# A two-block transformer kernel: banks of the wide products, and the engine and place of a blocked substitution

## The chip, the cores and the metric

One core of a Trainium2 chip runs the whole program in one launch. The metric is the time on the device in microseconds (us); lower is better. Three runs of the kernel before gave 936.17, 937.05 and 939.07 us, median 937.05. Engines: TensorE multiplies (PE in the profile, PEld its weight loads), VectorE (DVE), ScalarE (ACT) and GpSimd (POOL) do elementwise work, SyncE (SP) issues most DMA transfers. Each engine runs its own queue strictly in order.

## The reference, cut to what matters

The input is 256 tokens of 1024 numbers, in float32. Two transformer blocks follow each other. The first has an attention with 8 heads, beside it a gated delta rule with 8 heads in chunks of 64 tokens, an output projection and an MLP of width 4096. The second has a short convolution branch, a retention branch, three output projections and a gated MLP of width 2816.

The change touches two places. The first is the delta rule's triangular solve, which is done for each of 32 units (8 heads by 4 chunks):

```python
m = jnp.where(strict, jnp.einsum('bhnid,bhnjd->bhnij', k_beta, kc) * decay, 0.0)
a_mat = m + jnp.eye(C, dtype=jnp.float32)            # C = 64
uw = lax.linalg.triangular_solve(a_mat, rhs, left_side=True, lower=True, unit_diagonal=True)
```

The second is every projection whose result is wanted with channels on the partitions, such as the MLP's `square(relu(h @ w_up))`.

## The kernel before, in words

**Precision and weights.** Each float32 product is made of reduced-precision ones: an operand is split into a high part H and a rest L, and H times H, H times L and L times H are summed. `load_w` (L207 on) does this for 512 KB of weights at a time: a DMA on SP's queue fills `raw` (3 buffers), ScalarE writes `wh` as a copy of it, VectorE writes `wl` as `raw` minus `wh` (6 buffers each). This pair of instructions, called a split below, occurs 287 times; the nth split is the nth call. `GATE_H` and `GATE_L` tie the first few to instructions that they must follow.

**The wide products.** `gemm_wide` (L300) makes 128 output channels for all 256 tokens in one step of sixteen matmuls: eight with 512 moving columns (the high and low part of the activations side by side) and eight with 256. The result is one PSUM bank. ScalarE copies its second half out and VectorE adds the first half; then the bank is free. There are 84 such steps in the program: 24 in the first MLP, 24 in the convolution branch, 36 in the second MLP. All take their bank from `mmps()`, which goes round 3 banks (`BANKS = {"mm": 3, "sd": 3, "at": 2}`). `atps()` goes round 2 more, which the attention, the transposes of a normed row and one group of a head use.

**The substitution.** Each unit's 64x64 matrix is inverted in blocks. Its 128 diagonal blocks of 16x16 go, one for each partition, through DRAM: `m` is written to `md`, and `mb` is read back with a block in each partition's 256 columns. Fifteen steps of forward substitution follow; step j multiplies 15-j rows by j+1 columns and subtracts. The inverse `tb` and its transpose `ub` are written to DRAM (`td`, `ud`) and read back as `T` and `U` in the layout of units (L937 to L943). Two rounds of 64x64 products on TensorE with the masked matrices `b` (for block sizes 16 and 32, L947 on) then complete the inverse. The first of these products has the operands `U` and `b`.

**What sets the order.** The program is written as one stream: a main line (the delta rule) and a generator `side` of other work (the projections, the attention) from which `go(n)` takes pieces with a total of n. `FILL` holds these n. The framework puts each engine's instructions in its queue by a list scheduler that follows the written order among what its own estimate takes to be ready, so neighbours can change places. `after(name)` forbids an instruction to stand ahead of the instruction recorded under that name on the same engine; a name that is not recorded yet has no effect.

Counting the calls of `load_w` along the stream: split 13 is the last ahead of the substitution's lines (L884 on), splits 14 to 17 belong to `FILL[6]` to `FILL[8]`, split 18 (first half of `att_in(1)`) to `FILL[9]` at L944, split 19 (its second half) to `FILL[10]`, splits 20 to 23 to the gate projection `z_in`.

Of the kernel before, what the change touches and what calls it, by code (L numbers as in the profile page):

```python
# [11 lines left out]
F32 = mybir.dt.float32  # L12
F32R = mybir.dt.float32r
AF = mybir.ActivationFunctionType
# [23 lines left out]
GATE_L = ("xs", "xl", "xl", None, "g")  # L38
TAIL = 4
FILL = (1.3, 2.6, 3.9, 7.8, 1.3, 2.6, 1.3, 3.9, 3.9, 2.6, 2.6, 7.8, 2.6, 7.8)  # L40
# [57 lines left out]
def body(ctx: ExitStack, tc: tile.TileContext, I: dict, cst: bass.AP, out: bass.AP, dbg=None):  # L98
    nc = tc.nc
    P = 128  # L100

    def dump(name, ap):
        if dbg is not None:
            dbg(name, ap)
# [10 lines left out]
    def nm(s):  # L115
        uid[0] += 1
        return f"{s}_{uid[0]}"
# [4 lines left out]
    def G2(name, dt=F32, shape=None):  # L122
        return T2(name, dt, shape, "g")
# [7 lines left out]
    def bank(tag):  # L131
        return psum.tile([P, 512], F32, tag=tag, name=nm(tag), bufs=BANKS[tag])

    def mmps():
        return bank("mm")

    def sdps():
        return bank("sd")

    def atps():  # L140
        return bank("at")

    def act(o, i, f, **kw):
        nc.scalar.activation(o, i, f, **kw)  # L144

    def tt(o, a, b, op, eng=None):
        (eng or nc.vector).tensor_tensor(o, a, b, op=op)  # L147
# [4 lines left out]
    MUL, ADD, SUB, MAX = ALU.mult, ALU.add, ALU.subtract, ALU.max  # L152
# [14 lines left out]
    last, started = {}, []  # L167

    @contextmanager
    def after(what):  # L170

        if what in last:
            with tc.issue_after(last[what].ins):
                yield
        else:
            yield
# [26 lines left out]
    def C(name):  # L203
        o, w = COFF[name]
        return CT[o // 512][:, o % 512:o % 512 + w]


    def load_w(w, k0, nk, c0, ncol):
        raw = wpool.tile([P, nk, ncol], F32, tag="raw", name=nm("raw"), bufs=RBUFS)
        nc.sync.dma_start(raw, w[k0 * P:(k0 + nk) * P, c0:c0 + ncol].rearrange("(k p) n -> p k n", p=P))  # L210
        H = wpool.tile([P, nk, ncol], F32R, tag="wh", name=nm("wh"), bufs=WBUFS)
        L = wpool.tile([P, nk, ncol], F32R, tag="wl", name=nm("wl"), bufs=WBUFS)
        n = len(started)
        started.append(1)
        with after(GATE_H[n] if n < len(GATE_H) else None):
            act(H, raw, AF.Copy)
        with after(GATE_L[n] if n < len(GATE_L) else None):
            tt(L, raw, H.bitcast(F32), SUB)
        return H, L

    def mm(o, a, b, start=True, stop=True):
        nc.tensor.matmul(o, a, b, start=start, stop=stop)  # L222
# [34 lines left out]
    def gemm_tok_steps(w, c0, X, evac):  # L257

        ps = [mmps() for _ in range(2)]
        for q in range(4):  # L260
            H, L = load_w(w, 2 * q, 2, c0, 512)
            for t in range(2):
                for k in range(2):
                    kk = 2 * q + k
                    mm3(ps[t], *X.at(kk, t), H[:, k, :], L[:, k, :], kk == 0, kk == 7)
            if q == 3:
                for t in range(2):
                    evac(t, ps[t])
            yield 2.6
# [7 lines left out]
    def piece():  # L277
        for it in list(later):
            it[0] -= 1
            if it[0] <= 0:  # L280
                later.remove(it)
                it[1]()

    def gemm_ch_steps(w, c0, X, evac):

        ps = mmps()
        for f in range(2):
            H, L = load_w(w, 0, 8, c0 + f * P, P)
            o = ps[:, f * 256:(f + 1) * 256]
            for k in range(8):  # L290
                XH, XL = X.at(k)
                mm(o, H[:, k, :], XH, k == 0, False)
                mm(o, H[:, k, :], XL, False, False)
                last["step"] = nc.tensor.matmul(o, L[:, k, :], XH, start=False, stop=k == 7)  # L294
            if f == 1:
                evac(ps)
            piece()
            yield 2.6

    def gemm_wide(w, c0, X, o, then=None):  # L300


        for f in range(2):
            H, L = load_w(w, 0, 8, c0 + f * P, P)
            ps = mmps()
            for k in range(8):
                mm(ps, H[:, k, :], X.both(k), k == 0, False)
                mm(ps[:, :S], L[:, k, :], X.at(k)[0], False, k == 7)
            half = o[:, f * S:(f + 1) * S]
            act(half, ps[:, S:], AF.Copy)  # L310
            tt(half, ps[:, :S], half, ADD)
            if f == 1 and then:
                then()
            piece()
# [57 lines left out]
    def gemm_k(w, nk, X, *a):  # L372
        return GemmK(w, nk).finish(X, *a)
# [136 lines left out]
    def h8(ap):  # L510
        return ap.rearrange("p (h d) -> p h d", h=8)
# [8 lines left out]
    def cb(name):  # L520

        return C(name)[:, None, :].to_broadcast([P, 8, 64])
# [165 lines left out]
    def go(what):  # L688

        while what not in passed if isinstance(what, str) else what > 0:  # L690
            c = next(side, None)
            if c is None:
                return
            if isinstance(c, str):
                passed.add(c)
            elif not isinstance(what, str):
                what -= c
# [10 lines left out]
    H, L = load_w(w_in, 0, 8, 3584, 16)  # L708
# [101 lines left out]
    md, td, ud = (dram.tile([128, BS], F32, name=n) for n in ("md", "td", "ud"))  # L810
# [6 lines left out]
    def in_blocks(d):  # L817

        d = d[:, :]
        return bass.AP(tensor=d.tensor, offset=d.offset, ap=[[BS, P], [64, 16], [1, 16]])  # L820


    KBE, KD, KT_, MM, BL = [], [], [], [], []
# [61 lines left out]
    tb, ub, mb, tmp = (z_.rearrange("p (i j) -> p i j", i=16) for z_ in (tb_, ub_, mb_, tmp_))  # L885
    nc.gpsimd.tensor_copy(tb_, C("eye16"))
    nc.sync.dma_start(mb, in_blocks(md))
    for j in range(15):
        n, w = 15 - j, j + 1
        tt(tmp[:, :n, :w], mb[:, j + 1:, j:j + 1].to_broadcast([P, n, w]),  # L890
           tb[:, j:j + 1, :w].to_broadcast([P, n, w]), MUL, nc.gpsimd)
        tt(tb[:, j + 1:, :w], tb[:, j + 1:, :w], tmp[:, :n, :w], SUB, nc.gpsimd)
    last["sub"] = nc.gpsimd.tensor_copy(ub, tb.rearrange("p i j -> p j i"))
    nc.sync.dma_start(in_blocks(td), tb)
    nc.sync.dma_start(in_blocks(ud), ub)
    for t in range(2):
        bl = []
        for s in (16, 32):
            b = G2("b")
            with after("sub"):  # L900
                tt(h8(b), h8(MM[t]), cb(f"lev{s}"), MUL, nc.gpsimd)
            bl.append(b)
        BL.append(bl)

# [29 lines left out]
        VB.append(vb)  # L934
    go(FILL[8])

    U, T = [None] * 2, [None] * 2  # L937
    for t in range(2):
        T[t], U[t] = G2("T"), G2("U")
# [1 line left out]
            for c in range(2):  # L941
                nc.sync.dma_start(h8(o)[c * 64:(c + 1) * 64], in_units(d, t, c))
        dump(f"u16{t}", U[t])  # L943
    go(FILL[9])  # L944
    for si, s in enumerate((16, 32)):
        q, pt = [None] * 2, [None] * 2
        for t in range(2):  # L947
            ps = sdps()
            b, u0 = BL[t][si], U[t]
# [66 lines left out]
    for t in range(2):  # L1016
        po = sdps()
        vn = USB[t]
        for c in range(2):
            n = 2 * t + c  # L1020
# [43 lines left out]
    ps = wout.ps  # L1064
# [22 lines left out]
    for i in range(4, 16):  # L1087
        hf = G2("hf")

        def up_evac(i=i, hf=hf):  # L1090
            r = G2("relu")
            act(r, hf, AF.Relu)
            stt(hf, hf, 0.0, r, MAX, MUL)
            hv = hf.rearrange("p (j n) -> p j n", j=2)
            act(hid.h[i], hv, AF.Copy)
            tt(hid.l[i], hv, hid.h[i].bitcast(F32), SUB)

        gemm_wide(I["w_up"][0], 256 * i, X, hf, up_evac)
# [14 lines left out]
    ps = gemm_k(I["w_down"][0], 32, hid, TAIL_DOWN)  # L1113
# [45 lines left out]
    for h in range(4):  # L1159
        ps = sdps()  # L1160
# [33 lines left out]
    for h in range(4):  # L1194
        for t in range(2):
            ps = sdps()
# [25 lines left out]
    for i in range(4):  # L1222
# [9 lines left out]
        for j in range(2):  # L1232
            f = 2 * i + j
# [24 lines left out]
    ps = gemm_k(I["w_a_out_2"][0], 8, cv, TAIL_A)  # L1258
# [5 lines left out]
    ps = gemm_k(I["w_r_out_2"][0], 16, yr, TAIL_R)  # L1264
# [10 lines left out]
    ps = gemm_k(I["w_o_2"][0], 8, mg, TAIL_O)  # L1275
# [40 lines left out]
    ps = down.ps  # L1316
# [8 lines left out]
    for n, g in enumerate(down.parts[1]):  # L1325
        gs = down.cols[g]
        w = gs.stop - gs.start
# [49 lines left out]
```

## Time and profile before

| what | value |
|---|---|
| median of three runs | 937.05 us |
| profiled execution, its own time | 940.04 us |
| its span, first to last instruction | 937.9 us |
| PE busy | 904.9 us (96%) |
| PE weight loads busy | 771.3 us (82%) |
| VectorE busy | 595.1 us (63%) |
| ScalarE busy | 476.4 us (51%) |
| GpSimd busy | 93.2 us (10%) |
| mean granted TensorE clock | 0.991 |

The span is the time from the first to the last instruction; the profiled execution's own time adds 2.1 us around it and is 3.0 us above the median. Busy time is an engine's time inside instructions. [...] A wait is idle time of an engine directly before an instruction, put down to what ended last.

### The profile page before, as it was taken

The page shows a single profiled execution, that of the slowest core. Times are in us where ns is not written, and L with a number is a line of the kernel's source. Part 1 is how long each engine was busy: PE and PEld are TensorE (multiplying, and loading weights), DVE is VectorE, ACT ScalarE, POOL GpSimd, SP SyncE. Part 2 cuts the span into 40 slices and gives each one's busy share as a digit, 9 for nine tenths or more (in the row PEclk, how much of TensorE's full clock was granted, in tenths as well). Part 3 has the DMA queues.
Part 4 walks back from the last instruction along what each step waited for, and adds up shares of the span by engine and source line. Part 5 has one row for each costly group of instructions (what it writes and reads, how often), then busy time and mean ns, then how long its engine had stood idle before and what let it go on. Part 6 is the DMA issues. An engine that isn't in the chain of part 4 may idle for free.

```text
span 937.9 us, 13888 instructions
## 1 busy us (share of the span) xinstructions
PE 904.9 (96%) x5397; PEld 771.3 (82%) x5397; DVE 595.1 (63%) x855; ACT 476.4 (51%) x721; POOL 93.2 (10%) x127
## 2 busy tenths in 40 slices
PE   5999899999899999999999999999999999999997
PEld 4789687777788888799988888888888788888886
DVE  3887445476777564768666677754557657666543
ACT  4775263255666453555445565444344446555432
POOL 4068001030000000203200000000000000000000
PEclk9999899999999999999999999999999999999999
DMA  9666642146665666487645467666474567666551
GB/s 278 184 187 140 158 125 90 45 147 188 184 193 186 215 202 198 129 236 210 192 135 157 116 177 202 194 189 200 142 240 137 174 193 212 187 190 188 182 178 45
DMA packets 177137, 162.41 MB, mean 173 GB/s; under 512 B 18940, under 2 KB 144168, under 8 KB 177072
## 3 DMA queue, kind: packets, MB, share of 16 engines
q1 hardware_dynamic: 175200, 156.49, 57.4%
q0 software_dynamic: 1728, 4.78, 1.6%
q8 instruction: 42, 0.69, 0.3%
q10 hardware_dynamic: 144, 0.26, 0.1%
q14 instruction: 23, 0.19, 0.1%
HBM read 158.59 MB, written 2.92 MB: 172 GB/s over the span
## 4 chain that ended last, share of the span: by engine, by line
PE 81%; DMA 7%; DVE 3%; ACT 3%; issue 3%; POOL 2%; SPq 0%; POOLq 0%; ACTq 0%; DVEq 0%
PE mm L222 65%; PE at L222 7%; PE sd L222 6%; DMA raw<-in_w_in_dram 2%; PE mm L294 2%; DMA raw<-in_w_up_dram 2%; DVE wl L147 1%; ACT wh L144 1%; POOL tb L147 1%; DVE acc L150 1%; POOL tmpb L147 1%; DMA hs<-in_dec_b_dram 1%; ACT junk L421 1%; DMA U<-ud 1%; DMA wb<-in_pre_mix_norm_dram 1%
## 5 line engine op out<-in xcount | busy, mean ns | idle before, releaser
L147 DVE TENSOR_TENSOR wl<-raw,wh 128x1024 fp32r<-128x1024 f32 (+1 forms) x287 | 350.7, 1225 | 226.6 <-ACT wh L144 224.1
L144 ACT ACTIVATE wh<-raw 128x1024 fp32r<-128x1024 f32 (+1 forms) x287 | 302.1, 1056 | 310.0 <-PE mm L222 91.6
L222 PE MATMUL mm<-xT,wh 128*128 128x512 f32 (+1 forms) x1248 | 345.7, 348 | 4.1 <-DVE hf L147 2.5
L222 PEld LDWEIGHTS mm<-xT,wh 128*128 128x128 f32 x1248 | 217.9, 191 | 36.1 <-DVE hf L147 2.8
L222 PE MATMUL mm<-xT,wl 128*128 128x256 f32 x672 | 188.6, 281 | 0.0
L222 PE MATMUL mm<-wh,xT 128*128 128x512 f32 x528 | 169.2, 395 | 2.7 <-DVE xT L413 1.5
L222 PEld LDWEIGHTS mm<-xT,wl 128*128 128x128 f32 x672 | 127.4, 190 | 0.0
L222 PEld LDWEIGHTS mm<-wh,xT 128*128 128x128 f32 x528 | 99.2, 189 | 25.8 <-DVE xT L413 2.8
L222 PE MATMUL mm<-wl,xT 128*128 128x512 f32 x264 | 103.7, 393 | 0.0
L294 PE MATMUL mm<-xT,wl 128*128 128x256 f32 x288 | 82.3, 286 | 1.3 <-DVE wl L147 1.3
L222 PE MATMUL mm<-wh,hidh 128*128 128x512 f32 x162 | 63.4, 391 | 0.0
L222 PE MATMUL mm<-wl,hidh 128*128 128x512 f32 x162 | 63.2, 390 | 0.0
L222 PE MATMUL mm<-wh,hidl 128*128 128x512 f32 x162 | 63.0, 389 | 0.0
L222 PEld LDWEIGHTS mm<-wl,xT 128*128 128x128 f32 x264 | 49.9, 189 | 10.2 <-DVE wl L147 0.4
L294 PEld LDWEIGHTS mm<-xT,wl 128*128 128x128 f32 x288 | 55.7, 193 | 1.8 <-DVE wl L147 1.8
L425 POOL TENSOR_TENSOR r<-ms,neghalf 128x1 f32<-128x1 f32 x13 | 10.7, 823 | 435.2 <-DVE ms L150 435.2
L222 PEld LDWEIGHTS mm<-wh,hidl 128*128 128x128 f32 x162 | 30.4, 188 | 6.5
L222 PEld LDWEIGHTS mm<-wh,hidh 128*128 128x128 f32 x162 | 30.5, 188 | 6.3 <-DVE hf L147 0.3
L222 PEld LDWEIGHTS mm<-wl,hidh 128*128 128x128 f32 x162 | 30.5, 188 | 5.5
L147 DVE TENSOR_TENSOR hf<-mm,hf 128x256 f32<-128x256 f32 x42 | 17.5, 419 | 8.7 <-ACT hf L144 8.7
L147 POOL TENSOR_TENSOR rotl<-rot,roth 128x512 fp32r<-128x512 f32 x8 | 14.5, 1808 | 52.5 <-ACT roth L144 52.5
L421 ACT ACTIVATE junk<-x 128x512 f32<-128x512 f32 x18 | 11.3, 626 | 16.5 <-DVE x L147 12.0
(365 smaller groups left out, 1174.2 us busy)
## 6 DMA issues: line engine op xcount, KB each, us to landing
raw<-in_w_in_dram SPq DMA_DIRECT2D x116, 512.0 KB, 4.4
raw<-in_w_up_dram SPq DMA_DIRECT2D x32, 512.0 KB, 4.1
raw<-in_w_down_dram SPq DMA_DIRECT2D x32, 512.0 KB, 3.5
raw<-in_w_ff_gate_dram SPq DMA_DIRECT2D x22, 512.0 KB, 4.4
raw<-in_w_ff_up_dram SPq DMA_DIRECT2D x22, 512.0 KB, 3.8
raw<-in_w_ff_down_dram SPq DMA_DIRECT2D x22, 512.0 KB, 3.5
raw<-in_w_r_out_dram SPq DMA_DIRECT2D x16, 512.0 KB, 3.7
raw<-in_w_out_dram SPq DMA_DIRECT2D x8, 512.0 KB, 3.5
```

The costliest lines, as they stand in the source:

```text
L144: nc.scalar.activation(o, i, f, **kw)
L147: (eng or nc.vector).tensor_tensor(o, a, b, op=op)
L150: nc.vector.scalar_tensor_tensor(o, a, s, b, op0=op0, op1=op1)
L222: nc.tensor.matmul(o, a, b, start=start, stop=stop)
L294: last["step"] = nc.tensor.matmul(o, L[:, k, :], XH, start=False, stop=k == 7)
L421: last["sq"] = nc.scalar.activation(T2("junk", tag="j"), srcs[i], AF.Square, scale=1.0 / 32, accum_out=ss[:, i:i + 1])
L425: last["pow"] = nc.gpsimd.tensor_tensor(r, ms, neghalf[:, :1], op=ALU.pow)
```

## The change

1. `gemm_wide` counts its steps; steps whose count modulo 5 is 2 or 4 take their bank from `atps()`, the others from `mmps()`. The 84 steps go round five banks.
2. The substitution's 30 multiplications and subtractions go from GpSimd to VectorE. They are written later: behind the values' transposes (`VB`), `FILL[8]` and `FILL[9]`, which moves up from behind the loads of `U` and `T`. The last subtraction is recorded as `sub`; the multiplications must follow the last VectorE split written so far (the 18th), and every later split on VectorE must follow `sub`.
3. The transposing copy to `ub` goes from GpSimd to ScalarE; the stores of `td` and `ud` move along. The masked products `b` on GpSimd no longer follow the substitution.

```diff
-        with after(GATE_L[n] if n < len(GATE_L) else None):
-            tt(L, raw, H.bitcast(F32), SUB)
+        with after(GATE_L[n] if n < len(GATE_L) else "sub"):
+            last["wl"] = nc.vector.tensor_tensor(L, raw, H.bitcast(F32), op=SUB)
...
+    wide = []
...
-            ps = mmps()
+            wide.append(1)
+            ps = atps() if len(wide) % 5 in (2, 4) else mmps()
...
-    for j in range(15):
-        n, w = 15 - j, j + 1
-        tt(tmp[:, :n, :w], mb[:, j + 1:, j:j + 1].to_broadcast([P, n, w]),
-           tb[:, j:j + 1, :w].to_broadcast([P, n, w]), MUL, nc.gpsimd)
-        tt(tb[:, j + 1:, :w], tb[:, j + 1:, :w], tmp[:, :n, :w], SUB, nc.gpsimd)
-    last["sub"] = nc.gpsimd.tensor_copy(ub, tb.rearrange("p i j -> p j i"))
-    nc.sync.dma_start(in_blocks(td), tb)
-    nc.sync.dma_start(in_blocks(ud), ub)
...
-            with after("sub"):
-                tt(h8(b), h8(MM[t]), cb(f"lev{s}"), MUL, nc.gpsimd)
+            tt(h8(b), h8(MM[t]), cb(f"lev{s}"), MUL, nc.gpsimd)
...
     go(FILL[8])
+    go(FILL[9])
+    for j in range(15):
+        n, w = 15 - j, j + 1
+        with after("wl"):
+            tt(tmp[:, :n, :w], mb[:, j + 1:, j:j + 1].to_broadcast([P, n, w]),
+               tb[:, j:j + 1, :w].to_broadcast([P, n, w]), MUL)
+        last["sub"] = nc.vector.tensor_tensor(tb[:, j + 1:, :w], tb[:, j + 1:, :w], tmp[:, :n, :w], op=SUB)
+    nc.sync.dma_start(in_blocks(td), tb)
+    act(ub, tb.rearrange("p i j -> p j i"), AF.Copy)
+    nc.sync.dma_start(in_blocks(ud), ub)
...
-    go(FILL[9])
```

## Rows read from the trace of the kernel before

**Rows 1.** Waits of PE over the span: waiter, releaser: us in total, times, longest.
```profile
PE sd L222 <- DMA U<-ud: 4.5, 1, 4.5
PE mm L222 <- DVE hf L147: 2.5, 1, 2.5
PE sd L222 <- DVE m L147: 1.3, 1, 1.3
```
**Rows 2.** Windows: us, busy us (x) of PE, PEld, DVE, ACT, POOL, PEclk, DMA, GB/s.
```profile
60.00:65.00 5.00, 3.71 (x39) 3.64 (x40) 5.00 (x12) 2.66 (x4) 4.81 (x4) 1.00 0.94 252
72.90:97.20 24.30, 20.89 (x207) 19.33 (x205) 18.88 (x27) 13.24 (x22) 18.50 (x35) 1.00 0.62 158
98.30:104.70 6.40, 6.39 (x41) 4.62 (x42) 3.22 (x9) 1.86 (x8) 0.00 (x0) 0.50 1.00 209
237.50:241.20 3.70, 3.66 (x12) 3.09 (x13) 2.81 (x5) 1.93 (x5) 0.00 (x0) 0.54 0.58 162
250.00:300.00 50.00, 50.00 (x284) 43.21 (x283) 37.95 (x53) 32.81 (x54) 0.00 (x0) 1.00 0.64 188
```
**Rows 3.** Timeline of PE between the third and fourth wide step.
```profile
234.74 0.28 PE L222 MATMUL mm<-xT,wl 128*128 128x256 f32 x1
237.54 0.58 PE L222 MATMUL mm<-xT,wh 128*128 128x512 f32 x1 [2.52 <-DVE hf L147]
```
**Rows 4.** Timeline of ACT before that: first wide step's copy behind a split.
```profile
234.84 1.06 ACT L144 ACTIVATE wh<-raw 128x1024 fp32r<-128x1024 f32 x1 [3.13 <-DMA raw<-in_w_up_dram]
235.80 0.36 ACT L144 ACTIVATE hf<-mm 128x256 f32<-128x256 f32 x1
```
**Rows 5.** Timeline of DVE: the fourth step's split, and the first step's addition.
```profile
229.28 1.22 DVE L147 TENSOR_TENSOR wl<-raw,wh 128x1024 fp32r<-128x1024 f32 x1
237.07 0.42 DVE L147 TENSOR_TENSOR hf<-mm,hf 128x256 f32<-128x256 f32 x1
```
**Rows 6.** Timeline of POOL: substitution from first to last of 30, then `b`.
```profile
72.82 0.22 POOL L147 TENSOR_TENSOR tmpb<-mb,tb 128x15 f32<-128x15 f32 x1 [0.29 <-DMA mb<-md]
73.12 1.10 POOL L147 TENSOR_TENSOR tb<-tb,tmpb 128x15 f32<-128x15 f32 x1
...
87.82 0.22 POOL L147 TENSOR_TENSOR tb<-tb,tmpb 128x15 f32<-128x15 f32 x1
88.67 5.06 POOL L147 TENSOR_TENSOR b<-m,cs 128x512 f32<-128x512 f32 x4
```
**Rows 7.** Timeline of DVE beside the substitution: splits 18 and 19, later work.
```profile
68.22 1.21 DVE L147 TENSOR_TENSOR wl<-raw,wh 128x1024 fp32r<-128x1024 f32 x1
72.64 0.29 DVE L147 TENSOR_TENSOR fqd<-fq,ec 128x8 f32<-128x8 f32 x2
72.88 1.24 DVE L147 TENSOR_TENSOR wl<-raw,wh 128x1024 fp32r<-128x1024 f32 x1
92.53 1.28 DVE L619 TENSOR_SCALAR lg<-lg,rse 128x128 f32<-128x128 f32 x1
103.98 0.28 DVE L619 TENSOR_SCALAR lg<-lg,rse 128x128 f32<-128x128 f32 x1
```
**Rows 8.** Timeline of DVE: a small instruction and the next one, which reads it.
```profile
214.42 0.20 DVE L502 RECIPROCAL lpr<-lpw 128x8 f32<-128x8 f32 x1
214.65 0.17 DVE L147 TENSOR_TENSOR lpd<-lpd,lpr 128x8 f32<-128x8 f32 x1
```
**Rows 9.** Chain of waits between the substitution and TensorE: start, us, what.
```profile
88.75 3.92 DMA ud<-ub
92.72 5.44 DMA U<-ud
```
**Rows 10.** Timeline of PE up to the first U product: start, us, instruction [idle before <-releaser].
```profile
80.56 1.57 PE L222 MATMUL at<-aqk,aqk 64*128 64x128 f32 x8
...
92.87 0.92 PE L222 MATMUL at<-aqk,aqk 64*128 64x128 f32 x4
98.31 0.44 PE L222 MATMUL sd<-U,b 64*64 64x64 f32 x2 [4.52 <-DMA U<-ud]
```

## The prediction

> **What bounds the kernel now.** I read the page's busy times first: PE is busy for 904.9 of 937.9 us, so the time can fall only where PE stands still or runs at its lower clock. Then PE's waits over the span [rows 1]: apart from the start-up, two are longer than 2 us. One is 4.5 us for `U`, the inverse of the 16-blocks on its way back from DRAM; the other is 2.5 us for `hf`, VectorE's addition that empties a bank of a wide product. Each half of the change is aimed at one of them. [...]
>
> So each wait has two terms. For `U`: 4.52 us of standing still and 6.40 x 0.50 = 3.2 us lost to the clock, 7.7 us in all. For `hf`: 2.52 + 3.70 x 0.46 = 4.2 us. Together 11.9 us, and no other wait of PE bears on the edits. In the rest of the wide stages there is nothing to win: from 250 to 300 us PE is busy for 50.00 of 50.00 us at 1.00 [rows 2].
>
> **Part 1, five banks.** The reader should follow why the fourth wide step waits. With three banks it needs the bank of the first. That bank's copy on ScalarE stands behind a split whose weights came late (ScalarE idled 3.13 us for them), so it starts at 235.80 and VectorE's addition ends at 237.49; PE, done with step three at 235.0, starts at 237.54 [rows 3 to 5]. The fourth step's own weights were split by 230.5 [rows 5]. After the change the fourth step takes a bank of the other pair. Its last user there was a group of the MLP's head that ran before the first wide step, so the bank is empty. What is late next is step four's successors: the split that ScalarE did at 234.84 is for step six, its VectorE half follows at about 236 to 237.2, and step six would start at 235.0 + 2 x 2.8 = 240.6 (a step is eight pairs; 284 matmuls in 50 us give 2.8 us for sixteen). That is 3 us of slack. I take the full 4.2 us. Bounds: 0 if the order of the queues puts another late split in front, 4.2 if nothing does. Elsewhere the five banks cost nothing, since the steps already follow each other without a gap.
>
> **Part 2, the substitution.** On GpSimd its 30 instructions run from 72.82, when `mb` lands, to 88.04: 15.2 us. Some are stretched: a subtraction of 15 columns takes 1.10 us at 73.12, while VectorE does split 19, and another of 15 columns 0.22 us at the end [rows 6, 7].
>
> On VectorE I work it out from two sizes: 1024 columns take 1.21 to 1.24 us [rows 7], 8 columns 0.17 us [rows 8], which makes 0.16 us fixed and 1.04 ns a column. An instruction that reads its predecessor's result starts 0.03 us after that one's end (0.23 us after its start, with 0.20 us duration) [rows 8]. All 30 form one chain. Step j has (15-j)(j+1) columns, 680 in all, twice: 1360 x 1.04 ns = 1.4 us; 30 x (0.16 + 0.03) = 5.7 us. Sum 7.1 us. From below: two independent 8-column instructions took 0.29 us together [rows 7], a pitch of 0.12 us; 30 x 0.12 + 1.4 = 5.0 us. From above: GpSimd and VectorE hold each other up (a scaling took 1.28 us on VectorE beside `b`, and 0.28 us later without it [rows 7]); `b`, 5.06 us on GpSimd [rows 6], is no longer tied to the substitution and might run beside it: 7.1 + 5.1 = 12.2 us. I take 7.1, because `b`'s inputs are ready before `mb` is, so it will mostly be done.
>
> [...]
>
> Where it stands: the 18th split ended at 69.4 and the 19th began at 72.88 [rows 7], and `mb` lands at 72.8. The piece fits into that joint: 72.8 to 79.9. It is followed by the copy to `ub` on ScalarE (a 256-column copy takes 0.36 us [rows 4]; with a gap or a split ahead of it, 0.6 to 1.4), the store 3.92 and the load 5.44 us [rows 9], and 0.3 us of starts: `U` is there at about 90.1. With the bounds of the piece, 88 to 95.2. PE came to the first `U` product at 93.8 [rows 10]. So the wait goes, with 3.7 us to spare; at the late end 1.4 us of it stay, as long as the wait near 60 us that cost no clock [rows 2].
>
> What the piece displaces: VectorE's work behind it. The 19th split and all later ones start 7 us later, as does what the scheduler puts behind them, such as the scalings to `qn`. From 72.9 to 97.2 VectorE was busy for 18.88 of 24.30 us [rows 2], which leaves 5.4 us. Scalings that `b` held up give back about another 2 us, an estimate (1.0 us in the row shown, doubled for those beside it). The 7.1 us fit almost exactly, so VectorE is full in this stretch, and every eviction there can be late for PE. PE's cover: the products of split 18, the logits, and from 82 us on also those of splits 19 and 20. SP's queue: the stores of `td` and `ud` wait at its head for the piece instead of for GpSimd, with weight loads behind them, but those need a buffer that a late split frees, so little more is held back. Cost on PE between 0 (all of it fits) and 5 us (7.1 less what idles, all of it hit by one late eviction and some clock); I take 2.
>
> Part 2 then brings 7.7 - 2 = 5.7 us, and with part 1 9.9 us. The profiled execution (span 937.9, own time 940.04) would become 930.1; it is 3.0 us above the median of the runs, so the forecast is 937.05 - 9.9 = 927.1 us.
>
> **The rivals.**
>
> *The wait for `U` stays.* The order in PE's queue is made from estimates, and a substitution that is estimated shorter may pull the `U` products forward by as much as the data come earlier. For it: before, the order expected `U` 4.5 us too early. Against it: most of GpSimd's excess came from the stretched instructions, and these go. Only the banks help: 937.05 - 4.2 = 932.9.
>
> *The bank wait stays in another form.* A late load of weights then stops PE directly, for 0 to 4.2 us. For it: ScalarE's idle 3.13 us [rows 4]. Against: 3 us of slack for step six. Time 937.05 - 5.7 = 931.4.
>
> *Slower: the first `U` product stands so early that PE blocks on it.* PE's queue is in order, so everything behind it waits, and nothing of `side` can step in. If PE comes to it ahead of the first logits, at 80.6 [rows 10], and `U` lands at the late end, 95.2, PE waits 14.6 us and loses 3.2 to the clock: 17.8 - 7.7 - 4.2 = +5.9, or 943. It decides from a wait of 8.7 us on (8.7 + 3.2 = 11.9). For it: `U`'s products are written ahead of `FILL[10]`. Against: before, they stood behind logits that are written after `FILL[10]` [rows 10], so the estimate had `U` late.
>
> *Nothing net*: both waits go and the full VectorE gives the time back. 937.
>
> [...]
>
> **How the numbers follow.** Chances: forecast 0.55; `U`'s wait stays 0.15; the bank wait 0.08; nothing net 0.08; the blocked queue 0.12; the clock 0.02. The forecast's own span is 924.9 (no new wait: 937.05 - 11.9 = 925.1) to 930.1 (5 us of them). The range to 936 takes in the two smaller gains and part of the no-change case; below, 924 leaves 1 us for what the model of the piece may miss. A measurement of this kernel tells 0.3%, 2.8 us, from no change. The first three cases lie beyond it nearly always: faster 0.75, within 0.10, slower 0.15.
>
> **What would show it.** Right: VectorE's timeline has 30 small instructions in one piece of about 7 us from about 73 us, `ub` on ScalarE near 80, `U` landing near 90; among PE's waits neither `U` nor `hf` appears; the granted clock is 1.00 at 98 to 105 and at 237 to 241. Wrong: PE waits for `qn`, a split or an eviction between 80 and 95 for over 5 us, or for `U` at an earlier place; a piece of over 12 us; a clock below 1.00 in the wide stages.

## The result and the profile after

The changed kernel took 932.28 us (median; 929.5 to 934.4), the kernel before 938.64 us in the same comparison: a ratio of 0.994, 95% interval 0.9926 to 0.9954. It is faster, by 4.8 us against the median of 937.05 that the forecast started from and by 6.4 us in the comparison; the forecast was 9.9. The time lies between the forecast's bounds of 924 and 936, but the gain is only half to two thirds of the one forecast. A second set of runs (below, after_again) gave 0.9938.

PE's waits after the change, in the columns of [rows 1]:

```profile
PE sd L222 <- DVE m L147: 1.3, 1, 1.3
PE sd L795 <- DVE qn L147: 1.2, 1, 1.2
PE at L632 <- DVE lg L150: 0.6, 1, 0.6
PE sd L222 <- DMA U<-ud: 0.6, 1, 0.6
```

The wait for `hf` is gone. The wait for `U` is down from 4.5 to 0.6 us, and two small waits on VectorE (`qn`, and `lg`, a scaling of logits) are new.

Two windows give a ledger that serves all that follows: 57 to 110 us holds the work around the substitution, 225 to 260 us the head of the first MLP. The stall of a window is its length less PE's busy time, plus busy time multiplied by one less the granted clock (PEclk, TensorE's rate as a share of its full one). The rows of the kernel before, in the columns of [rows 2]:

```profile
57.00:110.00 53.00, 47.16 (x460) 42.09 (x459) 38.60 (x67) 26.74 (x47) 30.54 (x43) 0.94 0.70 170
225.00:260.00 35.00, 31.57 (x173) 26.98 (x172) 26.71 (x38) 22.55 (x39) 0.00 (x0) 0.95 0.69 194
```

The same windows after, and three inside them:

```profile
57.00:110.00 53.00, 49.45 (x518) 44.47 (x518) 41.40 (x94) 25.21 (x47) 19.18 (x12) 0.97 0.61 141
60.00:65.00 5.00, 3.68 (x34) 3.43 (x33) 5.00 (x12) 2.41 (x4) 5.00 (x6) 0.84 0.91 244
65.00:70.00 5.00, 5.00 (x37) 5.00 (x37) 5.00 (x6) 2.70 (x4) 5.00 (x4) 0.82 0.82 183
95.00:100.00 5.00, 4.39 (x36) 3.40 (x36) 3.31 (x9) 1.66 (x2) 0.00 (x0) 1.00 1.05 205
225.00:260.00 35.00, 34.60 (x199) 30.20 (x200) 27.70 (x41) 23.23 (x40) 0.00 (x0) 1.00 0.74 207
```

Substitution stage before: 53 - 47.16 + 47.16 x 0.06 = 8.7 us of stall; after, 3.55 + 1.5 = 5.0. MLP stage: 3.43 + 1.6 = 5.0 before, 0.4 after. The clock behind the `U` product is now 1.00, but at 60 to 70 us, behind the wait of 1.3 us for `m` that cost no clock in [rows 2], it is 0.84 and 0.82.

**The banks** do what was said. Timeline of PE and VectorE at the fourth wide step (`at` is the other pair's bank), against [rows 3, 5]:

```profile
231.51 0.40 PE L222 MATMUL at<-xT,wh 128*128 128x512 f32 x1
...
233.13 0.42 DVE L147 TENSOR_TENSOR hf<-mm,hf 128x256 f32<-128x256 f32 x1
```

Step four starts without a wait. The first step's bank is emptied only by the addition at 233.13, which ends 2 us after that start: with three banks, PE would have stood here.

**The substitution** does not stand where it was put. Timeline of GpSimd, then of VectorE, against [rows 6, 7]:

```profile
64.98 8.00 POOL L147 TENSOR_TENSOR b<-m,cs 128x512 f32<-128x512 f32 x4
72.94 3.24 POOL L147 TENSOR_TENSOR rnq<-ms,neghalf 128x8 f32<-128x8 f32 x2
```

```profile
69.51 2.32 DVE L218 TENSOR_TENSOR wl<-raw,wh 128x1024 fp32r<-128x1024 f32 x1
76.37 0.68 DVE L147 TENSOR_TENSOR qn<-sd,fq 128x512 f32<-128x512 f32 x1
...
78.84 0.17 DVE L147 TENSOR_TENSOR tmpb<-mb,tb 128x15 f32<-128x15 f32 x1
...
81.57 1.08 DVE L147 TENSOR_TENSOR at<-sd,eu 128x256 f32<-128x256 f32 x3
83.29 0.42 DVE L147 TENSOR_TENSOR at<-sd,eu 128x256 f32<-128x256 f32 x1 [0.52 <-PE sd L222]
...
85.60 1.29 DVE L147 TENSOR_TENSOR vb<-sd,beta 128x512 f32<-128x512 f32 x2
...
88.66 0.17 DVE L937 TENSOR_TENSOR tb<-tb,tmpb 128x15 f32<-128x15 f32 x1
88.75 2.36 DVE L218 TENSOR_TENSOR wl<-raw,wh 128x1024 fp32r<-128x1024 f32 x2
```

`b`, no longer tied, ran ahead of `rnq` on GpSimd, and `qn` on VectorE waited for `rnq`. The piece begins behind `qn` at 78.84, is broken by six evictions, one of which waited for PE, and ends at 88.83: 10.0 us, of which its own 30 instructions, from start to start with the evictions and waits left out, are about 7.2. On GpSimd it had ended at 88.04 [rows 6]. What follows, on ScalarE, in the chain of waits and on PE, against [rows 9, 10]:

```profile
88.87 0.67 ACT L144 ACTIVATE ub<-tb 128x256 f32<-128x256 f32 x1 [6.99 <-DVE tb L937]
```

```profile
89.57 3.86 DMA ud<-ub
93.44 4.19 DMA U<-ud
97.62 0.14 issue
```

```profile
97.76 0.30 PE L222 MATMUL sd<-U,b 64*64 64x64 f32 x2 [0.60 <-DMA U<-ud]
```

`U` came at 97.62, hardly earlier than before (98.2), not at 90.1. The wait shrank because PE came to the product 3.4 us later (97.16 instead of 93.8), and not after more work: 600 matmuls stand ahead of the product in PE's queue, 601 before. From 57 us to the product PE stood still for 2.9 us instead of 1.3 (the wait for `qn` is the new one), and it lost 1.7 us to the clock, by 1-us windows, instead of none. So of the 7.1 us that the wait for `U` and the clock behind it gave up in this profile, 3.3 went to waits and clock ahead of it.

### The profile page after: what moved, and what is told of

The parts are those of the page before. It is cut to its first block, busy times and chain, and to the rows that moved or that the text cites. A ratio compares the mean times of both kernels' runs of the same rounds, so it can differ in the third digit from the quotient of the medians.

```text
span 930.4 us, 13880 instructions
## 1 busy us (share of the span) xinstructions
PE 902.0 (97%) x5397; PEld 770.2 (83%) x5397; DVE 600.1 (64%) x885; ACT 475.2 (51%) x722; POOL 81.2 (9%) x96
## 4 chain that ended last, share of the span: by engine, by line
PE 85%; DMA 4%; POOL 3%; ACT 3%; DVE 3%; issue 2%; SPq 0%; POOLq 0%; ACTq 0%
PE mm L222 57%; PE at L222 18%; PE sd L222 6%; PE mm L294 2%; DMA raw<-in_w_in_dram 1%; POOL b L147 1%; ACT junk L424 1%; DVE wl L218 1%; PE sd L795 1%; POOL r L428 1%; DMA rows<-in_w_conv_dram 1%; DMA raw<-in_w_up_dram 1%; ACT wh L144 1%; DMA wb<-in_pre_mlp_norm_dram 1%; DMA x<-in_x_dram 0%
## 5 line engine op out<-in xcount | busy, mean ns | idle before, releaser
L222 PE MATMUL mm<-xT,wh 128*128 128x256 f32 (+1 forms) x976 | 251.5, 334 | 1.4 <-ACT wh L144 1.4
L222 PEld LDWEIGHTS mm<-xT,wh 128*128 128x128 f32 x976 | 167.2, 193 | 21.0 <-ACT wh L144 1.6
L222 PE MATMUL mm<-xT,wl 128*128 128x256 f32 x400 | 111.9, 280 | 0.0
L222 PE MATMUL at<-xT,wh 128*128 128x512 f32 x272 | 97.4, 398 | 0.0
L294 PE MATMUL mm<-xT,wl 128*128 128x256 f32 x288 | 82.9, 288 | 1.2 <-DVE wl L218 1.2
L222 PE MATMUL at<-xT,wl 128*128 128x256 f32 x272 | 76.1, 280 | 0.0
L222 PEld LDWEIGHTS mm<-xT,wl 128*128 128x128 f32 x400 | 75.4, 189 | 0.0
L222 PEld LDWEIGHTS at<-xT,wh 128*128 128x128 f32 x272 | 51.1, 188 | 12.4
L294 PEld LDWEIGHTS mm<-xT,wl 128*128 128x128 f32 x288 | 56.5, 196 | 1.6 <-DVE wl L218 1.6
L222 PEld LDWEIGHTS at<-xT,wl 128*128 128x128 f32 x272 | 51.3, 189 | 0.0
```

## The experiments

Ratios are to runs of the kernel before on the same chip, with 95% intervals.

**1. Each half alone.** `banks_only` is the kernel before with five banks; `sub_only` the changed kernel with three:

```diff
...
-            ps = atps() if len(wide) % 5 in (2, 4) else mmps()
+            ps = mmps()
...
```

> Only the five banks of the wide products; the substitution as before. If the two halves add up, PE's wait for hf near 235 us goes and with it the stretch at half clock: 4.2 us off the kernel before (ratio 0.9955), while the wait of 4.5 us for U stays. Rival, the banks carry the whole gain: 6 us off (ratio 0.9935). Rival, they carry nothing and the gain is the substitution's: ratio 1.000.

> Only the substitution's move; three banks as before. If the halves add up: about 2 us off the kernel before (ratio 0.998), the wait for U under 1 us and the waits for qn and the half clock as in the changed kernel, the wait of 2.5 us for hf still there. Rival, the substitution carries it: 6 us off (0.9935). Rival, it loses: ratio over 1.001.

Banks alone: 934.54 us, 0.9978 (0.9964 to 0.9992). The substitution alone: 937.24 us, 1.000 (0.9982 to 1.0018). Neither half is worth what was forecast for it when alone. The profile of `banks_only`, waits and windows:

```profile
PE sd L222 <- DMA U<-ud: 5.0, 1, 5.0
```

```profile
57.00:110.00 53.00, 47.21 (x434) 42.18 (x433) 39.04 (x67) 27.00 (x47) 31.04 (x43) 0.90 0.70 170
225.00:260.00 35.00, 34.18 (x198) 29.52 (x197) 28.00 (x40) 22.79 (x39) 0.00 (x0) 1.00 0.71 199
```

The MLP stage stalls for 0.8 us instead of 5.0, the gain of 4.2 that was forecast; in this execution the substitution stage lost more than before (5.8 + 4.7 = 10.5). The waits of `sub_only`:

```profile
PE sd L792 <- DVE qn L147: 2.8, 1, 2.8
PE mm L222 <- DVE hf L147: 2.7, 1, 2.7
...
PE sd L222 <- DMA U<-ud: 0.7, 1, 0.7
```

The wait for `U` goes here too, and one of 2.8 us for `qn` takes part of its place.

**2. Is it `b`?** `b_after_sub` writes `b` behind the substitution and ties it to the copy `ub`, which goes back to GpSimd. `b_after_rnq` only makes `b` follow `rnq`:

```diff
-        tt(o, ms, neghalf[:, :n], ALU.pow, nc.gpsimd)
+        last["rstd"] = nc.gpsimd.tensor_tensor(o, ms, neghalf[:, :n], op=ALU.pow)
...
-            tt(h8(b), h8(MM[t]), cb(f"lev{s}"), MUL, nc.gpsimd)
+            with after("rstd"):
+                tt(h8(b), h8(MM[t]), cb(f"lev{s}"), MUL, nc.gpsimd)
```

> The changed kernel, but the masked products b follow the substitution on GpSimd again, by way of the copy to ub, which goes back to GpSimd. Theory A, that b ahead of rnq on GpSimd is what held the piece back: rnq ends near 72.7 instead of 76.2, the piece starts near 75.5 instead of 78.8, U lands near 94 instead of 97.6, PE's waits for qn (1.25) and U (0.6) go, and the time is 2 to 3 us under the changed kernel (ratio to before 0.991). Theory B, that VectorE is full and PE pays elsewhere whatever starts earlier: within 1 us of the changed kernel (0.994).

> The changed kernel, but b only has to follow both rnq on GpSimd, so it runs beside qn and the piece. Theory A: rnq ends near 72.7 and qn near 75.5 as when b follows the substitution, but the piece and b hold each other up, so the piece takes 2 to 5 us longer; time 1 to 2 us under the changed kernel. Theory B: within 1 us of the changed kernel.

931.58 us, 0.9945 (0.9933 to 0.9957), and 931.79 us, 0.9941 (0.9929 to 0.9954): no better than the changed kernel. The theory that `b` ate the gain falls. The timelines of GpSimd and VectorE in `b_after_rnq` show why:

```profile
68.44 4.14 POOL L403 TENSOR_TENSOR rnq<-ms,neghalf 128x8 f32<-128x8 f32 x2 [3.56 <-DVE ms L402]
```

```profile
76.33 0.17 DVE L147 TENSOR_TENSOR tmpb<-mb,tb 128x15 f32<-128x15 f32 x1
...
86.85 0.17 DVE L938 TENSOR_TENSOR tb<-tb,tmpb 128x15 f32<-128x15 f32 x1
```

`rnq` is done at 72.6, as before, and the piece starts 2.5 us earlier than in the changed kernel; but that is 76.33, still 3.5 us behind the forecast, and it ends at 87.02. It stands behind `qn` and `qd` and among the evictions in VectorE's own queue.

**3. Is the stall what one profile shows?** Two more profiles of the kernel before, and one of `sub_only` (sub_look).

> The kernel before, unchanged, a second profiled execution, because the first one (940.04 us) lies 3 us above the median of 18 others (937.12). Theory A, the stalls are the kernel's and only what surrounds them varies: the waits for U (4.5) and hf (2.5) and the half clock behind each stand again within 0.5 us. Theory B, the profiled execution was an unlucky one and overstated what the change could remove: in a typical execution the stretch for hf and its clock, 4.2 us, is 1 us or more shorter.

> A third profiled execution of the kernel before. Theory A: as before_look1. Theory B: the sum of wait and lost clock near 235 us differs by over 1 us between the three, and the time follows it.

> The substitution alone, a second profiled execution (its 12 runs went from 932.6 to 941.7 us). Theory A, its gain of 2.2 us in the first profile is real and the ends of the range are the clock's: the landmarks (first product with the values near 130.0, the norm near 194.8) repeat within 0.5 us and only the granted clock differs elsewhere. Theory B, what it wins is lost at the wide products' banks: the wait for hf near 235 us is longer than 2.7 us when the norm comes earlier.

PE waited for `U` 2.8 and 3.8 us instead of 4.5. The two windows of the first profile, then of the second:

```profile
57.00:110.00 53.00, 48.63 (x486) 43.81 (x482) 37.74 (x66) 26.73 (x47) 29.61 (x42) 0.94 0.72 177
225.00:260.00 35.00, 32.52 (x179) 28.07 (x178) 26.36 (x37) 21.76 (x37) 0.00 (x0) 0.95 0.70 194
```

```profile
57.00:110.00 53.00, 47.87 (x457) 43.01 (x456) 37.33 (x66) 26.54 (x46) 29.88 (x43) 0.90 0.69 169
225.00:260.00 35.00, 31.48 (x173) 27.00 (x172) 26.74 (x38) 22.27 (x39) 0.00 (x0) 0.95 0.68 187
```

Stalls: 7.3 and 9.9 us in the substitution stage, 4.1 and 5.1 in the MLP's. The bank's stall is steady (mean of three 4.7); the other moves from 7.3 to 9.9 (mean 8.6), because the clock loss moves too: in both it was below 1.00 at 60 to 65 us (0.67 and 0.77). Counting the wait for `U` and the clock loss behind it alone, from 1-us windows, the three profiles give 7.7, 4.5 and 6.4. The forecast took the highest. `sub_look`, 935.61 us, had 1.3 us for `qn` and 0.5 for `U`; its wait for the bank was 2.7 us again, and so not longer, as theory B had it.

**4. Without the rule between splits and substitution.** `no_gates`:

```diff
-        with after(GATE_L[n] if n < len(GATE_L) else "sub"):
+        with after(GATE_L[n] if n < len(GATE_L) else None):
...
-        with after("wl"):
-            tt(tmp[:, :n, :w], ...
+        tt(tmp[:, :n, :w], ...
```

> The changed kernel without the two orderings between the substitution and the splits (no split has to follow it, and it has to follow none); the order then puts five splits into the piece. Theory A, the gates matter: the piece ends 6 us later (five splits of 1.2 us), U lands near 103 and PE waits for it 3 us or more: 3 us over the changed kernel (ratio to before 0.997). Theory B, PE's own order adapts, as it stands 23 matmuls later: within 1 us of the changed kernel (0.994).

928.18 us, 0.990 (0.9877 to 0.9923): some 4 us better than the changed kernel. The second half of the edit changes nothing: without it alone, every engine's instructions keep the order of the changed kernel. All comes from letting later splits pass. VectorE's and PE's timelines, then a wait of PE and the window:

```profile
79.71 0.18 DVE L147 TENSOR_TENSOR tmpb<-mb,tb 128x15 f32<-128x15 f32 x1
79.80 1.22 DVE L218 TENSOR_TENSOR wl<-raw,wh 128x1024 fp32r<-128x1024 f32 x1
...
97.03 0.17 DVE L936 TENSOR_TENSOR tb<-tb,tmpb 128x15 f32<-128x15 f32 x1
```

```profile
104.72 0.29 PE L222 MATMUL sd<-U,b 64*64 64x64 f32 x2 [0.32 <-DMA U<-ud]
```

```profile
PE sd L795 <- DVE qn L147: 2.8, 1, 2.8
```

```profile
57.00:110.00 53.00, 48.94 (x458) 44.28 (x457) 45.39 (x99) 28.70 (x49) 20.05 (x13) 1.00 0.63 158
```

Five splits run inside the piece, which ends at 97.2, 8.4 us later, and yet the time falls. PE comes to the `U` product 7 us later and waits 0.3 us. The stage stalls for 4.1 us, all of it standing still. So the date at which `U` is ready does not set the time by itself. But the edit moved two things, the splits and the product's place.

**5. The place alone.** The kernel before with five banks and the substitution left on GpSimd. `gpsimd_u_later` takes more of the side stream's work ahead of the `U` products:

```diff
-FILL = (1.3, 2.6, 3.9, 7.8, 1.3, 2.6, 1.3, 3.9, 3.9, 2.6, 2.6, 7.8, 2.6, 7.8)
+FILL = (1.3, 2.6, 3.9, 7.8, 1.3, 2.6, 1.3, 3.9, 3.9, 9.1, 2.6, 7.8, 2.6, 7.8)
```

`gpsimd_sub_late` writes the substitution (and `b` with it) behind `FILL[9]`, as the change does, but on GpSimd and without the rule:

```diff
+    go(FILL[9])
     for j in range(15):
...
+           tb[:, j:j + 1, :w].to_broadcast([P, n, w]), MUL, nc.gpsimd)
...
-    go(FILL[9])
```

> The kernel before with five banks and the substitution left on GpSimd at its old place; only FILL[9] goes from 2.6 to 9.1, so that more side work is written ahead of the U products (PE's order has them 12 instructions later). Theory P, that U's wait is a matter of the place of the product in PE's queue and not of how soon U lands: the wait for U falls from 5 us to 2 or less and the half clock behind it goes, 4 us or more under the banks alone (ratio to before 0.9935 or less). Theory E, that the engine and the end of the substitution count: U lands at 98 as before, what PE does meanwhile is missing later, and the time stays at that of the banks alone (0.998).

> The kernel before with five banks and the substitution written at the new place (behind FILL[9]) but still on GpSimd, without gates; PE's order then has the first U product 21 instructions earlier than before. Theory P: PE comes to it near 90, U lands at 98 or later, the wait is 8 us or more and the time is 3 us or more over that of the banks alone (ratio to before 1.001 or more). Theory E: the end of the substitution stays near 88, so does the time of the banks alone (0.998).

`gpsimd_u_later`: 927.41 us, 0.9874 (0.9851 to 0.9897), by its ratio the fastest of all, with the substitution where it had been (15.4 us from the landing of `mb`, which in this execution came 2 us earlier than in [rows 6]). PE's timeline and the window:

```profile
96.36 0.29 PE L222 MATMUL sd<-U,b 64*64 64x64 f32 x2 [1.02 <-DMA U<-ud]
```

```profile
57.00:110.00 53.00, 50.79 (x561) 45.80 (x558) 40.26 (x69) 26.64 (x48) 29.67 (x44) 1.00 0.72 178
```

2.2 us of stall, against 10.5 in `banks_only`, from one number in a list. `gpsimd_sub_late` took 934.47 us, 0.9957 (0.9942 to 0.9973): its `U` product stands 21 places earlier in PE's queue (runs of like matmuls counted as one), and PE waits again. PE came to the product at 90.25, as theory P forecast, but the rest of that forecast missed: `U` landed at about 95.5 instead of 98, the wait was 5.4 us instead of 8, and the time is not over that of the banks alone (0.9978; the intervals overlap). So the earlier place kept the wait, but it did not cost more time.

```profile
95.67 0.44 PE L222 MATMUL sd<-U,b 64*64 64x64 f32 x2 [5.42 <-DMA U<-ud]
```

**6. Combinations.** `no_gates_b_after_sub` joins experiments 2 and 4, `no_gates_3_banks` takes the banks out of experiment 4.

> The changed kernel without gates, and with b behind the substitution on GpSimd (the copy to ub there again). Theory Q, that rnq's lateness now shows on PE as the wait of 2.8 us for qn: it falls under 1 us and the time is 1 to 2 us under the kernel without gates (ratio to before 0.9885). Rival: PE's order absorbs it as it did with the gates: ratio 0.990, within 0.001.

> The changed kernel without gates and with three banks. If the banks are worth 4.2 us in every combination, as the profiles of the MLP stage say, 932.5 us (ratio to before 0.9945), with the wait of 2.5 us for hf and the half clock behind it. Rival, what the substitution wins is lost at the banks when they are three, as the substitution's move alone gained nothing with gates: ratio 0.999 to 1.000.

927.39 us, 0.9884 (0.9863 to 0.9905), and 934.42 us, 0.9959 (0.9942 to 0.9976). The first beats both kernels, and its wait for `qn` is gone, as theory Q said; but its interval holds the rival's 0.990 too. The second lies near the forecast 0.9945 and not at the rival's 0.999, and has the bank's wait again:

```profile
PE mm L222 <- DVE hf L147: 2.4, 1, 2.4
```

Here the banks are worth the step from 0.9959 to 0.990, some 5.5 us.

**7. The place in the changed kernel.** `after_u_later` keeps the rule and puts work between the substitution's stores and the loads of `U`; `after_again` is the changed kernel beside it.

```diff
     nc.sync.dma_start(in_blocks(ud), ub)
+    go(6.5)
```

> The changed kernel with 6.5 more of the side stream's work written between the substitution's stores and the loads and products of U; the rule that later splits on VectorE follow the substitution is kept. Without that rule the changed kernel took 0.990 of the time before, with it 0.994, and the first U product stood 23 places later in TensorE's queue, so two causes were mixed. Theory G (splits held behind the substitution cost TensorE time): the rule is still there, so the ratio stays at 0.993 to 0.995, 931 to 933 us. Theory P (the later place of the U product is what paid): the ratio falls to 0.989 to 0.991, 927 to 929 us, though the splits still wait; TensorE's wait for U, 0.6 us in the changed kernel, is gone.

> The changed kernel as it is, on the same chip as the one with the later U product. Both theories: 0.994 of the kernel before, within 0.0015. It also gives a second profile of the changed kernel: if the clock loss behind the wait of 1.3 us near 60 us belongs to the change, the granted clock is again below 1.00 at 60 to 70 us; if it differs from one execution to the next, it may be 1.00 there.

928.79 us, 0.9909 (0.9883 to 0.9934), against 933.01 us, 0.9938 (0.9917 to 0.9959). The medians are 4.2 us apart, though the intervals overlap; theory P forecast it, and theory G did not. `after_again`, waits and windows:

```profile
PE sd L795 <- DVE qn L147: 2.8, 1, 2.8
...
PE sd L222 <- DMA U<-ud: 1.0, 1, 1.0
```

```profile
57.00:110.00 53.00, 47.76 (x451) 42.38 (x449) 39.43 (x91) 21.87 (x43) 17.19 (x11) 0.94 0.60 138
95.00:100.00 5.00, 4.00 (x33) 2.65 (x33) 2.79 (x5) 1.10 (x5) 0.00 (x0) 0.72 1.14 207
100.00:105.00 5.00, 5.00 (x26) 4.03 (x24) 1.19 (x5) 1.64 (x7) 0.00 (x0) 0.60 1.01 293
225.00:260.00 35.00, 34.40 (x199) 29.77 (x198) 26.98 (x41) 22.42 (x39) 0.00 (x0) 1.00 0.72 197
```

This is one part of what was missing. The wait for `U` was 1.0 us here, and the clock behind it fell to 0.72 and 0.60, 3.4 us by 1-us windows, as much as behind the wait of 4.5 us before. In the first profile of the same kernel a wait of 0.6 us had cost none (1.00 from 95 to 105 us). In `gpsimd_u_later` and `b_after_sub`, again, waits of 1.0 and 1.1 us for `U` cost none (1.00 there too). A small rest of the wait is thus not always a small rest of the stall. `after_u_later`, PE's timeline and the window:

```profile
100.46 1.15 PE L222 MATMUL sd<-U,b 64*64 64x64 f32 x32
```

```profile
57.00:110.00 53.00, 50.16 (x551) 45.11 (x552) 40.71 (x92) 26.25 (x47) 18.49 (x12) 0.97 0.59 139
```

PE comes to the product when `U` is there: no bracket behind the row, no wait. Over all runs of the two (mean span, split by the mean granted clock) the later place saves 0.8 us of clock (3.6 instead of 4.3) and 2.1 us beside it (924.1 instead of 926.1); so the profile with 3.4 us of clock loss is one of the worse ones.

## Why the prediction was half right

**What bounds the kernel: right.** PE's stalls were the whole store of gain. Taken over all runs, the span times one less the mean granted clock (the clock's loss) fell from 7.3 to 7.8 us (before, by comparison) to 4.3 and 4.7 (the changed kernel), some 3 us; the rest of the span fell by about 2 us. The forecast had about 5 and 5.

**Part 1, the banks: right in place and mechanism, and in size by the stage's stall.** Forecast 4.2 us; the MLP stage's stall fell from a mean of 4.7 (three profiles) to 0.5 (two profiles). By 1-us windows all six profiles with three banks stall there for 3.9 us or more, all ten with five banks for 0.8 or less. The times do not agree on the size: 2.6 us alone, with an interval that ends at 3.4 and so leaves out 4.2, and some 5.5 beside the substitution. Step six did not become late, as argued: from 225 to 260 us PE was busy for 34.6 of 35 us at 1.00.

**Part 2, the piece's own length: right.** 7.1 us forecast, about 7.2 measured without the evictions inside it; a pair of dependent instructions starts 0.21 to 0.26 us apart. By the forecast's 1.04 ns a column, some 5.8 of the 7.2 us go by the number of instructions, not of columns.

**Part 2, where it stands: wrong. This is the step that failed**: "The piece fits into that joint: 72.8 to 79.9." The joint was read off the old timeline as if the piece would enter it when `mb` lands. In VectorE's queue the piece stood behind `qn` and `qd` (76.37 to 78.92), and VectorE did not step over them: up to 76.21 it stood idle for 0.79 us until `rnq` was done, though `mb` had landed at 73.8. Six evictions stood inside it. The piece began at 78.84 and ended at 88.83, 9 us late; `U` came at 97.62 instead of 90.1. "`b` ... will mostly be done" failed too: `b` took 8.00 us instead of 5.06 and held `rnq` up. With `b` moved away the piece still began at 76.3, so `b` is 2.5 of the 6.0 us by which it began late, and the rest is what stands ahead of it in VectorE's queue.

**The stall's size: too large, and it did not go whole.** The wait for `U` with its clock was entered at 7.7 us, one profile's value (4.52 us still, then 6.40 us at a clock of 0.50; for `hf` 2.52, then 3.70 at 0.54 [rows 2]); three profiles give 7.7, 4.5 and 6.4, in the mean 6.2. In the changed kernel 0.6 and 4.4 us of it are left, in the mean 2.5, since `U` was still late. So 3.7 us went. The other stalls of the stage grew from 2.5 to 4.4 us in the mean, with the wait for `qn` among them: a cost on PE of 1.9 us where 2 were forecast, which with so few profiles is partly luck. The term "7.7 - 2 = 5.7" thus came out as 3.7 - 1.9 = 1.8 us; the ledger of the stage, 8.6 us before and 6.6 after (5.0 and 8.1), says 2.0. With the banks' 4.2 that makes about 6, near the medians (4.8 to 6.4). The forecast also let a wait of up to 1.4 us cost no clock, by the one row near 60 us; in five of the other profiles a wait of 1.2 to 1.6 us at that instruction cost 1.7 us of clock.

**What decides instead: the `U` product's place in PE's queue.** The forecast asked when the data come, and took PE's arrival, 93.8, as fixed. The runs moved both. PE did not step over the product: in `banks_only` it stood still ahead of it for 5.0 us, in `gpsimd_u_later`, with more work written ahead of it, for 1.02. Later data with a later place was faster (`no_gates`), the same data with a later place was faster with either engine (`gpsimd_u_later` clearly; `after_u_later` by medians, its interval overlaps). For an earlier place the case is weaker: `gpsimd_sub_late` has a wait of 5.4 us, but no longer time than the banks alone. In the changed kernel the product still stands on the edge, at the old place, so that 0.6 to 1.0 us of wait stay; behind the 1.0 us the clock fell to 0.72 and 0.60, behind the 0.6 us it stayed at 1.00.

**The rivals.** "The wait for `U` stays", 932.9, came nearest in time. Its mechanism is half of what happened: the product's place stayed as early as it was (600 matmuls ahead of it, 601 before), but it was not pulled forward, and the wait itself shrank. The blocked queue, as a mechanism, is what the forecast gave too little weight; here it did not cost time, it kept gain away, as the gain of `after_u_later` suggests. The chance of 0.02 for the clock stood for a granted clock below 1.00 in the wide stages with five banks; no run shows one: from 225 to 260 us it was 1.00 in all ten profiles with five banks, and in the changed kernel's first profile from 66.9 to 926.9 us.

**What stays open.** By medians the substitution alone is worth nothing, and 0.4% once the banks are there (0.994 against 0.9978); the banks alone 0.22%, and 0.6% beside either form of the substitution. The halves seem to help each other, though their stages lie 115 us apart; the ledgers don't show why. Nor do they show why `b_after_sub`, with 2.0 us of stall in its profile (2.01 idle at 1.00), was no faster than the changed kernel. A part of the second stands ahead of the stage: in its first 57 us that profile stalled for 16.3 us by 1-us windows, the changed kernel's two for 14.6 and 13.3. Chance in single profiles may be enough for the rest, but that was only argued. (The low end of the forecast's own span, given as 924.9, is 925.1 by its own sum; nothing hangs on it.)

## What to carry to other kernels

Ask first where the waiting instruction stands in its engine's queue and what could stand ahead of it; here, moving it back by a few microseconds of ready work cost one number and beat a faster producer (0.9874 against 0.994). An idle stretch in the old timeline is not a slot: list what the queue will put ahead of and inside the moved piece. Take a stall's size from several executions, with the clock behind it, and forecast that it goes only if the wait goes to zero with some margin.

## What the hardware showed beside

In these profiles the clock's fall is not proportional to the wait, nor the same for the same wait; where it cost nothing, the granted clock stayed at 1.00, elsewhere it fell to 0.50. Behind 4.5 us of waiting for `U` it cost 3.2 us, behind 1.0 us 3.4 in one profile and nothing in another (`gpsimd_u_later`), behind 0.6 us nothing. Behind the wait for `m` of 1.1 to 1.6 us it cost nothing in three profiles ([rows 2], `after_again`, `no_gates_3_banks`) and about 1.7 us in five others (0.84 and 0.82 above). Behind 2.8 us of waiting for `qn` it cost nothing in `no_gates` and `after_again`, and 1.7 us in `sub_only` and `no_gates_3_banks`.

GpSimd and VectorE took longer beside each other here too: four `b` of 512 columns took 8.00 us beside VectorE's splits and 5.06 us without them [rows 6], and a split took 2.32 us instead of 1.21 [rows 7].
